# Turning the gated values of SwiGLU with DMA transposes of two 16-bit planes instead of TensorE transposes

## The chip, the core and the metric

The kernel runs on one core of one Trainium2 chip. The metric is device time in microseconds (us) of one execution, the median of several runs. A profiled execution of the same kernel gives a trace of every instruction on TensorE (PE, with its weight loads as PEld), VectorE (DVE), ScalarE (ACT), GpSimd (POOL), and of the DMA queue that SyncE (SP) issues into.

## What is computed

A two-layer encoder over 256 tokens of width 1024, in float32. Each layer adds half a SwiGLU block, a mixer (attention) and another half SwiGLU block to x:

```python
def swiglu(h, w_gate, w_up, w_down):
    return (jax.nn.silu(h @ w_gate) * (h @ w_up)) @ w_down

def reference(x, ...):
    for layer in range(DEPTH):                      # DEPTH = 2
        h = rms_norm(x, ffn1_norm[layer])
        x = x + 0.5 * swiglu(h, ffn1_w_gate[layer], ffn1_w_up[layer], ffn1_w_down[layer])
        h = rms_norm(x, mix_norm[layer])
        x = x + (even_mixer if layer % 2 == 0 else odd_mixer)(h, ...)
        h = rms_norm(x, ffn2_norm[layer])
        x = x + 0.5 * swiglu(h, ffn2_w_gate[layer], ffn2_w_up[layer], ffn2_w_down[layer])
    return rms_norm(x, final_norm)
```

The hidden width of SwiGLU is 2816. The gated values, `silu(h @ w_gate) * (h @ w_up)`, come out with tokens on the partitions, and the product with `w_down` needs the hidden index on the partitions: each 128x128 block of them has to be turned.

## The kernel before

**Tiles.** The 256 tokens are two row tiles of 128 (`tt` 0 and 1). A float32 product is made of three TensorE products: operands are split into a high part and a low part (`hi`, `lo` of the weights; `th`, `tl` of the normalised input; `g_h`, `g_l` of the gated values), and `mm` issues hi*hi, lo*hi and hi*lo at lines 460 to 462, each 128x512. One such triple is called a step below.

**Stages.** Stages 0, 2, 3 and 5 are the four SwiGLU blocks, 1 and 4 the mixers. A SwiGLU stage goes through five chunks of 512 hidden columns and a last one of 256 (`FF_MIXED`): gate products for both row tiles, up products for both, then `silu` on ACT (line 649) and `glu` on DVE (line 654). After all chunks come the products with `w_down`.

**Strassen chunks.** In each stage one or two chunks (`SEVEN`: chunk 2 in stages 0 and 5, chunks 1 and 3 in stages 2 and 3), and some pairs of the down products, are made with seven instead of eight products. They need sums of weights: DVE makes `two` and rewrites `raw` (line 389), ACT makes `shi` and DVE `slo` from them, beside the usual `hi` and `lo`. So DVE does more work there for fewer steps of TensorE. The parts of the finished chunk are put together and gated on DVE at lines 754 to 792 (`L773` is the gating).

**Weights.** SP issues loads of the weights into three buffers `raw` (`load`, line 373), ACT rounds them to `hi` (line 468), DVE subtracts to `lo` (line 471). At most seven pairs `wp` and three pairs `sum` are held, so ACT waits for TensorE's last use of a pair when it is far ahead.

**What sets the order.** Every engine takes its instructions in the order in which the program writes them. Work that is not a product is written as generators: `tick` is called once after every step and advances each generator whose count of ticks has run out (`yield n` waits n ticks), then makes the next weight part when the due rate says so. Loops that only wait for a generator call `tick(False)`, which advances generators without a step of TensorE between them.

**The place of the change.** `glu` writes the gated tile `m`, waits `GLU_WAIT` = 14 ticks, and `transposed` turns its four blocks on TensorE into a PSUM bank `tp` (`turned`, line 538). ACT then copies out `quarters` (blocks that a Strassen pair of the down product needs, lines 680 and 683) and `g_h` (line 468), and DVE makes `g_l` (line 471).

Of the kernel before, what the change touches and what calls it, by code (L numbers as in the profile page):

```python
# [9 lines left out]
F32 = mybir.dt.float32  # L10
F32R = mybir.dt.float32r
BF16 = mybir.dt.bfloat16
AF = mybir.ActivationFunctionType
# [4 lines left out]
P = 128  # L18
# [7 lines left out]
ROWS = T // GRID_W  # L26
# [16 lines left out]
RAWS = 3  # L43
# [10 lines left out]
GLU_WAIT = 14  # L54
# [8 lines left out]
ROWS, ROWS_WAIT = 4, 30  # L63
# [64 lines left out]
class Split:  # L128
# [3 lines left out]
    def __init__(self, raw, uses, first=False, narrow=False, kind="wp", then=None):  # L132
        self.raw, self.first, self.narrow, self.kind, self.then = raw, first, narrow, kind, then
# [67 lines left out]
class Trunk:  # L201
# [161 lines left out]
    def load(self):  # L363
# [12 lines left out]
        if kind == "strassen":  # L376
            self.coming(self.strassen(raw, halves))
        else:
            views = [halves(raw[:, k, :]) for k in range(nk)] if w == D else [raw[:, k : min(k + 2, nk), :] for k in range(0, nk, 2)]
            self.coming([Split(view, uses, n == 0, kind == "narrow") for n, view in enumerate(views)])  # L380
# [5 lines left out]
    def strassen(self, raw, halves):  # L386
# [7 lines left out]
        def all_sums():  # L394
# [7 lines left out]
            Split(second[:, 0:1, :], [1], True, then=all_sums),  # L402
            Split(first, [1]),
            Split(first, [1], kind="sum"),
            Split(second, [1], kind="sum"),
# [3 lines left out]
    def supply(self):  # L409
# [6 lines left out]
        if split.parts is None:  # L416
            if split.first:
                self.load()
# [116 lines left out]
    def turned(self, src, n=4):  # L535
# [3 lines left out]
        return tb  # L539

# [95 lines left out]
    def ffn(self):  # L636
# [14 lines left out]
        def glu(tt, f0, w, u, s):  # L651
# [83 lines left out]
        def seven_gates(f0, w, pairs7):  # L735
# [12 lines left out]
            def common():  # L748
# [4 lines left out]
                w = self.t([P, 512], "silu", 2)  # L753
# [8 lines left out]
            def first_gate():  # L762
# [3 lines left out]
                s = self.t([P, 512], "silu", 2)  # L766
# [5 lines left out]
            def up(tt, o, u, s):  # L772
                nc.vector.scalar_tensor_tensor(o, u, self.now.r[tt], s, op0=ALU.mult, op1=ALU.mult)  # L773
                yield GLU_WAIT
                yield from transposed(tt, f0, w, o)
# [59 lines left out]
        for ci, w in enumerate(FF_CHUNKS):  # L835
# [11 lines left out]
            for tt in range(NT):  # L847
                g = both[tt] if self.now.n + ci == 0 else self.project(self.ready(tt), G, tags[tt])
                S.append(self.t([P, 512], "silu", 2))
# [8 lines left out]
        for tt in range(NT):  # L858
            both = self.project(self.now.hT[tt], V, "s")
            s = self.t([P, 512], "silu", 2)  # L860
# [49 lines left out]
        def combine():  # L910
# [5 lines left out]
            c = self.t([P, 512], "silu", 2)  # L916
# [3 lines left out]
            v = self.t([P, 512], "silu", 2)  # L920
# [5 lines left out]
            y = self.t([P, 512], "silu", 2)  # L926
# [328 lines left out]
    def fetch_row(self, rel, n):  # L1255

        row = self.little([P, 2, ROW], "rows", ROWS)
# [200 lines left out]
    def run(self):  # L1458
# [50 lines left out]
        self.rows = []  # L1509
        self.start(self.first_rows(a["c_rel_bias"][0]))  # L1510
        self.phase(self.ffn)
        self.next_stage()
        self.phase(self.odd, a["c_rel_bias"][0])
        self.next_stage()
# [31 lines left out]
```

## Time and profile before

| what | value |
|---|---|
| median of 3 runs | 954.43 us (954.36 to 954.94) |
| profiled execution, its own time | 954.08 us |
| its span in the trace | 952.3 us |
| PE busy | 939.0 us (99%) |
| DVE busy | 790.9 us (83%) |
| ACT busy | 583.2 us (61%) |
| DMA share of 16 engines, queue of SP | 53.9% |
| TensorE transposes of `glu` | 176, in 40 groups of four and 8 of two |

"Busy" is the union of an engine's instructions. PE's matmuls overlap in the records: one of 128x512 is shown with 0.39 us, and the next one starts about 0.23 us after it. Times of rows are counted from the span's start. A row of the timeline reads: start, duration, engine, line, operation, out<-in, shapes, count, and in brackets the idle time of the engine before it and what ended it.

### The profile page before, as it was taken

How to read it: one execution, taken by the hardware profiler on the slowest of the kernel's cores; microseconds unless marked ns; L12 is line 12 of the kernel's file. 1: busy time of each engine (PE TensorE's matmuls, PEld its weight loads, DVE VectorE, ACT ScalarE, POOL GpSimd, SP SyncE). 2: the span in 40 equal slices, each digit the busy share in tenths (PEclk: the TensorE clock that was granted, in tenths of full speed). 3: DMA queues.
4: the chain of work that ended last, by engine and by line, in shares of the span. 5: the costliest groups of instructions: out<-in, count | busy, mean ns of one | idle time of the engine just before them, and what ended most of it. 6: DMA issues, size and time to landing. Idle time of an engine off the chain costs nothing.

```text
span 952.3 us, 12568 instructions
## 1 busy us (share of the span) xinstructions
PE 939.0 (99%) x4575; PEld 770.2 (81%) x4575; DVE 790.9 (83%) x1228; ACT 583.2 (61%) x995; POOL 94.4 (10%) x152
## 2 busy tenths in 40 slices
PE   9999999999999999999999999999999999999997
PEld 6888888877878888888888888888878888888786
DVE  6989778788869998787978888888878697896797
ACT  7555655477787565645646556557777585555453
POOL 1120000063410000000100000006130000000001
PEclk9999999999999999999999999999999999999999
DMA  8737555644425665556446575664634365466261
GB/s 300 265 128 239 204 191 173 210 136 102 118 89 177 220 209 190 207 191 225 153 153 213 159 245 174 226 214 161 185 97 159 101 219 179 151 229 238 88 243 45
DMA packets 82751, 171.63 MB, mean 180 GB/s; under 512 B 4096, under 2 KB 17152, under 8 KB 82688
## 3 DMA queue, kind: packets, MB, share of 16 engines
q1 hardware_dynamic: 82112, 170.04, 53.9%
q8 instruction: 36, 0.59, 0.3%
q10 hardware_dynamic: 576, 0.79, 0.2%
q14 instruction: 27, 0.22, 0.1%
HBM read 169.76 MB, written 1.05 MB: 179 GB/s over the span
## 4 chain that ended last, share of the span: by engine, by line
PE 89%; DVE 5%; ACT 3%; issue 1%; DMA 1%; POOL 0%; POOLq 0%; ACTq 0%; DVEq 0%
PE s L461 12%; PE s L462 12%; PE s L460 12%; PE pj L460 12%; PE pj L462 11%; PE pj L461 11%; PE tp L538 2%; PE o L460 2%; PE o L462 2%; PE o L461 2%; DVE lo L471 2%; PE o L1019 2%; PE tp L1098 1%; PE tp L460 1%; PE tp L462 1%
## 5 line engine op out<-in xcount | busy, mean ns | idle before, releaser
L471 DVE TENSOR_TENSOR lo<-raw,hi 128x1024 fp32r<-128x1024 f32 (+1 forms) x372 | 374.2, 1027 | 64.2 <-ACT hi L468 61.4
L468 ACT ACTIVATE hi<-raw 128x1024 fp32r<-128x1024 f32 (+1 forms) x372 | 317.9, 890 | 76.4 <-PE s L462 26.3
L460 PE MATMUL s<-hi,th 128*128 128x512 f32 x373 | 149.1, 400 | 0.4 <-ACT hi L468 0.4
L460 PE MATMUL pj<-hi,th 128*128 128x512 f32 x367 | 146.7, 400 | 0.0
L461 PE MATMUL s<-lo,th 128*128 128x512 f32 x373 | 145.8, 391 | 0.3 <-DVE lo L471 0.2
L462 PE MATMUL s<-hi,tl 128*128 128x512 f32 x373 | 145.9, 391 | 0.0
L461 PE MATMUL pj<-lo,th 128*128 128x512 f32 x367 | 143.2, 390 | 0.1
L462 PE MATMUL pj<-hi,tl 128*128 128x512 f32 x367 | 143.3, 390 | 0.0
L461 PEld LDWEIGHTS s<-lo,th 128*128 128x128 f32 x373 | 70.2, 188 | 15.0 <-DVE lo L471 1.5
L462 PEld LDWEIGHTS s<-hi,tl 128*128 128x128 f32 x373 | 70.0, 188 | 14.9
L460 PEld LDWEIGHTS s<-hi,th 128*128 128x128 f32 x373 | 70.1, 188 | 13.9 <-ACT hi L468 0.6
L462 PEld LDWEIGHTS pj<-hi,tl 128*128 128x128 f32 x367 | 68.9, 188 | 14.7
L460 PEld LDWEIGHTS pj<-hi,th 128*128 128x128 f32 x367 | 69.0, 188 | 13.9 <-issue 0.9
L461 PEld LDWEIGHTS pj<-lo,th 128*128 128x128 f32 x367 | 69.1, 188 | 13.4 <-DVE lo L471 0.5
L480 POOL TENSOR_TENSOR rstd<-var,mhalf 128x1 f32<-128x1 f32 (+2 forms) x16 | 17.1, 1069 | 590.5 <-ACT th L501 309.0
L468 ACT ACTIVATE shi<-two 128x1024 fp32r<-128x1024 f32 x30 | 31.8, 1059 | 39.4 <-DVE two L389 39.3
L460 PE MATMUL s<-hi,g_h 128*128 128x512 f32 (+1 forms) x131 | 52.1, 398 | 0.0
L471 DVE TENSOR_TENSOR slo<-raw,shi 128x1024 fp32r<-128x1024 f32 x30 | 36.7, 1223 | 18.3 <-ACT shi L468 18.3
L468 ACT ACTIVATE shi<-raw 128x1024 fp32r<-128x1024 f32 x30 | 31.7, 1057 | 32.5 <-PE s L462 22.0
L468 ACT ACTIVATE g_h<-tp 128x512 fp32r<-128x512 f32 (+2 forms) x48 | 25.7, 537 | 42.4 <-DVE quarters L686 28.1
L462 PE MATMUL s<-hi,g_l 128*128 128x512 f32 (+1 forms) x131 | 51.0, 389 | 0.0
L461 PE MATMUL s<-lo,g_h 128*128 128x512 f32 (+1 forms) x131 | 50.8, 388 | 0.0
(483 smaller groups left out, 1668.4 us busy)
## 6 DMA issues: line engine op xcount, KB each, us to landing
raw<-in_ffn_w_down SPq DMA_DIRECT2D x44, 1024.0 KB, 5.0
raw<-in_ffn_w_up SPq DMA_DIRECT2D x28, 1024.0 KB, 5.2
raw<-in_ffn_w_gate SPq DMA_DIRECT2D x26, 1024.0 KB, 5.1
raw<-in_ffn_w_gate SPq DMA_DIRECT2D x35, 512.0 KB, 4.1
raw<-in_ffn_w_up SPq DMA_DIRECT2D x32, 512.0 KB, 5.1
raw<-in_odd_w_qkv SPq DMA_DIRECT2D x12, 1024.0 KB, 5.3
raw<-in_even_w_in SPq DMA_DIRECT2D x4, 1024.0 KB, 5.2
raw<-in_even_w_out SPq DMA_DIRECT2D x8, 512.0 KB, 6.0
```

The costliest lines, as they stand in the source:

```text
L460: mm(ps, h, wh, start=first, stop=False)
L461: mm(ps, h, wl, start=False, stop=False)
L462: mm(ps, l, wh, start=False, stop=last)
L468: self.nc.scalar.activation(hi, src, AF.Copy)
L471: self.nc.vector.tensor_tensor(lo, src, hi.bitcast(F32), op=ALU.subtract)
L480: nc.gpsimd.tensor_tensor(r[:, :n], v[:, :n], self.mhalf[:, :n], op=ALU.pow)
L538: self.nc.tensor.transpose(tb[:, i * P : (i + 1) * P], src[:, i * P : (i + 1) * P], self.ident)
L1019: self.nc.tensor.matmul(O[64 * s : 64 * s + 64, i * P : i * P + P], v(b0 + i, s, kc), pT[s][:, i, kc, :], start=(kc == 0), stop=(kc == 1),)
L1098: nc.tensor.transpose(tb[:, o : o + P], p[:, i, kc * P : kc * P + P], self.ident)
```

## The change

`turned` on TensorE is replaced, for the gated values alone, by `turned_over`. ACT copies the float32 tile `m` as 16-bit numbers into a new tile of the `silu` pool, all lower halves first and all upper halves behind (two planes of 512 columns). SP issues one DMA transpose of those 128x1024 16-bit numbers back into `m`, in eight blocks of 128x128. ACT copies `m` back into the other tile with lower and upper halves side by side again. The turned tile is then in SBUF, not PSUM, and `quarters` and the split into `g_h` and `g_l` read it there. `transposed` now runs as a generator of its own, so that waiting for the gating tasks no longer waits for the turning. The waits change from 14 ticks to 1 tick ahead of the first copy, 1 ahead of the DMA and 8 ahead of the second copy.

Two more edits go with it. The load of the next weights is written when the last part of a `raw` buffer has been made, not when the first part of a later one begins, and the first two such loads are left out because five were issued at the start; a load so stands in SP's queue near the time its buffer comes free. And the rows of the relative bias get a pool of their own, since `silu` has three buffers instead of two.

```diff
-GLU_WAIT = 14
+GLU_WAIT = 1
+TURN_WAIT = [1, 8]
...
+        self.ahead = len(FIRST) - RAWS
...
         if split.parts is None:
-            if split.first:
-                self.load()
...
+        if split.last and sl.stop == split.raw.shape[1]:
+            if self.ahead:
+                self.ahead -= 1
+            else:
+                self.load()
...
+    def turned_over(self, m, w):
+
+        two = self.t([P, 512], "silu", 3)
+        planes, back = (t.bitcast(U16)[:, : 2 * w] for t in (two, m))
+        self.nc.scalar.copy(planes.rearrange("p (h c) -> p h c", h=2), back.rearrange("p (c h) -> p h c", h=2))
+        yield TURN_WAIT[0]
+        self.nc.sync.dma_start_transpose(back.rearrange("p (j t) -> p j t", t=P), planes)
+        yield TURN_WAIT[1]
+        self.nc.scalar.copy(planes.rearrange("p (c h) -> p h c", h=2), back.rearrange("p (h c) -> p h c", h=2))
+        yield 1
+        return two
...
             nc.vector.scalar_tensor_tensor(m[:, :w], u[:, :w], self.now.r[tt], s[:, :w], op0=ALU.mult, op1=ALU.mult)
-            yield GLU_WAIT
-            yield from transposed(tt, f0, w, m)
+            self.spawn(transposed(tt, f0, w, m), GLU_WAIT)
...
         def transposed(tt, f0, w, m):
             n = w // P
-            tb = self.turned(m, n)
-            yield 1
+            tb = yield from self.turned_over(m, w)
...
             def up(tt, o, u, s):
                 nc.vector.scalar_tensor_tensor(o, u, self.now.r[tt], s, op0=ALU.mult, op1=ALU.mult)
-                yield GLU_WAIT
-                yield from transposed(tt, f0, w, o)
+                self.spawn(transposed(tt, f0, w, o), GLU_WAIT)
+                yield 1
...
-        row = self.little([P, 2, ROW], "rows", ROWS)
+        row = self.row_pool.tile([P, 2, ROW], F32, tag="rows", name=self.name("rows"), bufs=ROWS)
```

Three places of the order matter for what follows. The first is ACT in stage 2, at the end of chunk 0 and the start of the Strassen chunk 1. In the rows, `hi` and `shi` are weight parts, `g_0_h` the high part of the turned values of chunk 0 (one row for each row tile), the other `g_` and `k` rows sums of the input for the Strassen chunk. Before:

```order
L468 ACTIVATE hi_3152<-raw_2877 128x512
L468 ACTIVATE hi_3173<-raw_2877 128x1024
L468 ACTIVATE g_12_h_3183<-shi_3024 128x384
L468 ACTIVATE shi_3189<-two_3160 128x1024
L468 ACTIVATE g_16_h_3200<-shi_3024 128x384
L468 ACTIVATE k16h_3206<-slo_3072 128x384
L468 ACTIVATE g_0_h_3214<-tp_3209 128x512
L468 ACTIVATE k14h_3218<-slo_3072 128x384
L468 ACTIVATE shi_3230<-raw_2877 128x1024
L468 ACTIVATE hi_3244<-raw_2977 128x512
L468 ACTIVATE g_0_h_3255<-tp_3237 128x512
```

The same stretch of ACT in the changed kernel; COPY at L551 takes the halves apart, COPY at L555 puts them together:

```order
L474 ACTIVATE hi_3138<-raw_3068 128x512
L551 COPY silu_3156<-glu_3151 128x1024
L474 ACTIVATE hi_3162<-raw_3068 128x1024
L474 ACTIVATE g_12_h_3172<-shi_3010 128x384
L474 ACTIVATE shi_3178<-two_3146 128x1024
L474 ACTIVATE g_16_h_3189<-shi_3010 128x384
L551 COPY silu_3194<-glu_3192 128x1024
L555 COPY silu_3156<-glu_3151 128x2x512
L474 ACTIVATE g_0_h_3198<-silu_3156 128x512
L474 ACTIVATE k16h_3202<-slo_3055 128x384
L474 ACTIVATE k14h_3207<-slo_3055 128x384
L555 COPY silu_3194<-glu_3192 128x2x512
```

Behind these rows follow `g_0_h_3211` and `shi_3223`. The first COPY stands ahead of the last `hi` of its buffer, and both second COPYs stand ahead of the `shi` that was ninth before; between the COPY that feeds the second DMA transpose and the COPY that needs its result stand four short instructions, because a loop there waits for sums and advances generators without steps of TensorE.

The second is DVE at the same place in the changed kernel, where `slo_3224` is made from the `shi` just named:

```order
L672 SCALAR_TENSOR_TENSOR glu_3192<-pj_3141,rstd_3030,silu_3094 128x512
L477 TENSOR_TENSOR g_16_l_3190<-shi_3010,g_16_h_3189 128x384
L477 TENSOR_TENSOR g_0_l_3199<-silu_3156,g_0_h_3198 128x512
L477 TENSOR_TENSOR k16l_3203<-slo_3055,k16h_3202 128x384
L477 TENSOR_TENSOR k14l_3208<-slo_3055,k14h_3207 128x384
L477 TENSOR_TENSOR g_0_l_3212<-silu_3194,g_0_h_3211 128x512
L477 TENSOR_TENSOR slo_3224<-raw_3068,shi_3223 128x1024
```

Before, the second `g_0_l` stood five rows behind that `slo`; now both `g_0_l` stand ahead of it.

The third is ACT behind the Strassen chunk of stage 2, where `glu_3400` and `glu_3356` are its gated tiles, in the changed kernel:

```order
L551 COPY silu_3422<-glu_3400 128x1024
L474 ACTIVATE hi_3424<-raw_3354 128x1024
L804 ACTIVATE glu_3356<-glu_3356,rstd_3030 128x512
L551 COPY silu_3447<-glu_3356 128x1024
L667 ACTIVATE silu_3442<-pj_3391,rstd_2940 128x512
L474 ACTIVATE hi_3454<-raw_3354 128x1024
L474 ACTIVATE hi_3467<-raw_3378 128x1024
L555 COPY silu_3422<-glu_3400 128x2x512
```

Before, ACT went from the activation (`L788` there) straight to `silu` and three `hi`; now a COPY that needs the second gated tile stands between.

More of the change, by code (lines that the diff above doesn't have):

```diff
@@ L128, with __init__ @@
 class Split:
-    def __init__(self, raw, uses, first=False, narrow=False, kind="wp", then=None):
-        self.raw, self.first, self.narrow, self.kind, self.then = raw, first, narrow, kind, then
+    def __init__(self, raw, uses, last=False, narrow=False, kind="wp", then=None):
+        self.raw, self.last, self.narrow, self.kind, self.then = raw, last, narrow, kind, then
         n = raw.shape[1]
@@ L401, in strassen @@
         splits = [
[L402 removed]
+            Split(second[:, 0:1, :], [1], then=all_sums),
             Split(first, [1]),
             Split(first, [1], kind="sum"),
[L405 removed]
+            Split(second, [1], True, kind="sum"),
         ]
@@ L1508, in run @@
         self.next_stage()
[L1509 to L1514, printed above, removed]
+        with self.tc.tile_pool(name="rows", bufs=1, reuse_waits="tile") as self.row_pool:
+            self.rows = []
+            self.start(self.first_rows(a["c_rel_bias"][0]))
+            self.phase(self.ffn)
+            self.next_stage()
+            self.phase(self.odd, a["c_rel_bias"][0])
+            self.next_stage()
         self.phase(self.ffn)
```

17 lines of the change are left out of this document (9 added, 8 removed).

## The prediction

> **What bounds the kernel now.** I read the page's engine table and the shares of the chain that ended last first, then the timeline around a group of transposes, then the stretches in which DVE is fullest.
>
> ```profile
> span 952.3 us, 12568 instructions
> PE 939.0 (99%) x4575; PEld 770.2 (81%) x4575; DVE 790.9 (83%) x1228; ACT 583.2 (61%) x995; POOL 94.4 (10%) x152
> PE 89%; DVE 5%; ACT 3%; issue 1%; DMA 1%; POOL 0%; POOLq 0%; ACTq 0%; DVEq 0%
> ```
>
> PE is busy nearly without a gap and carries the chain, so time taken from PE is time taken from the end, as long as nothing else comes last. DVE has 17% left on the average, but not everywhere (stage 2, first 54 us; columns PE, PEld, DVE, ACT, POOL):
>
> ```profile
> 291.00:345.00 54.00, 53.67 (x244) 44.03 (x243) 52.39 (x63) 33.72 (x43) 0.00 (x0) 1.00 0.60 201
> ```
>
> Here DVE is busy 52.4 of 54 us: PE and DVE end together, and whatever makes DVE wait is a delay.
>
> **What is removed.** One group of four transposes in the stream of PE, and all of them in the tile's view:
>
> ```profile
> 35.00 0.39 PE L462 MATMUL s<-hi,tl 128*128 128x512 f32 x1
> 35.23 0.60 PE L538 MATMUL tp<-mats,glu 128*128 128x128 f32 x4
> 35.59 0.48 PE L460 MATMUL s<-hi,th 128*128 128x512 f32 x1
> 35.90 0.39 PE L461 MATMUL s<-lo,th 128*128 128x512 f32 x1
> L538 PE MATMUL tp<-mats,glu x176: 270/271/328, 35.2 to 897.4; 128*128 128x128 f32 x176
> ```
>
> A matmul follows the one ahead after 0.23 us (35.00 to 35.23). From 35.00 to 35.90 there are three such steps less one, 0.45 us, without the group; 0.90 are seen, so four transposes cost 0.45 us, 0.112 each (the 271 ns of the last row is a record that overlaps its neighbours). 176 x 0.112 = **19.7 us** come off PE. [...]
>
> **What is added on ACT.** Per tile of 512 columns two copies of 128x1024 16-bit numbers, for the tiles of 256 columns two of 128x512. Nearest rows:
>
> ```profile
> L468 ACT ACTIVATE hi<-raw 128x1024 fp32r<-128x1024 f32 x230 | 234.9, 1052 | 59.4 <-PE s L462 20.4 <-PE pj L462 17.8 <-DMA raw<-in_ffn_w_up 12.2
> L468 ACT ACTIVATE hi<-raw 128x512 fp32r<-128x512 f32 x142 | 85.1, 626 | 17.0 <-PE s L462 6.0 <-DMA raw<-in_ffn_w_down 4.1 <-DMA raw<-in_odd_w_qkv 3.8
> L468 ACT ACTIVATE g_h<-tp 128x512 fp32r<-128x512 f32 x30 | 17.8, 596 | 19.3 <-DVE quarters L686 10.7 <-PE tp L538 8.6
> ```
>
> No row has 16-bit operands on ACT. Same element count: 1.05 us; if two 16-bit numbers went as one, 0.63. I take 1.05, the row with the same number of elements. 80 x 1.05 + 16 x 0.63 = 94 us more on ACT, 677 in all, some 70%: as a sum it hides. `g_h` now reads SBUF, 626 for 596 ns, 48 times: 1.4 us, hidden too.
>
> **What is added on the queue of SP.** 48 DMA transposes, 11 MB to the 170 there. Nearest rows for one of 256 KB from issue to landing:
>
> ```profile
> out<-shi SPq DMA_DIRECT2D x2, 256.0 KB, 2.7
> rows<-in_c_rel_bias SPq DMA_DIRECT2D x16, 109.5 KB, 5.5
> last_gain<-in_final_norm SPq DMA_DIRECT2D x1, 512.0 KB, 7.2
> ```
>
> 2.7 is a plain transfer out of SBUF into an empty queue, 7.2 the longest of these. I take 6, near `rows`, which also goes in small pieces beside the weight loads. [...]
>
> The loads are written later, at the end of a buffer's use. I cost this at nothing: SP already stands waiting for exactly that event,
>
> ```profile
> SPq L373 <- DVE lo L471: 435.5, 106, 14.0
> ```
>
> so a load leaves when DVE frees its buffer, before and after. A DMA transpose ahead of it in the queue holds it until ACT's copy is done; the other two buffers cover that, and without them ACT's next `hi` would wait. The pool for the bias rows moves no work of the SwiGLU stages: nothing.
>
> **What is moved: where ACT now waits.** Before, ACT had `hi` and `shi` ready ahead of DVE, and `g_h` waited for PE only 14 ticks on. Now each first COPY waits on ACT for DVE's `glu`, with the `hi` and `shi` of the next weights queued behind it, on which DVE waits; each second COPY waits for a DMA. Stage 2, chunk 0, where the order was shown:
>
> ```profile
> 299.39 1.06 ACT L468 ACTIVATE hi<-raw 128x1024 fp32r<-128x1024 f32 x1 [3.12 <-PE pj L462]
> 301.40 0.74 DVE L654 SCALAR_TENSOR_TENSOR glu<-pj,rstd,silu 128x512 f32<-128x512 f32 x1
> 301.52 0.53 ACT L468 ACTIVATE g_h<-shi 128x384 fp32r<-128x384 f32 x1 [1.06 <-DVE shi L723]
> 301.95 1.05 ACT L468 ACTIVATE shi<-two 128x1024 fp32r<-128x1024 f32 x1
> 303.19 1.22 DVE L471 TENSOR_TENSOR slo<-two,shi 128x1024 fp32r<-128x1024 f32 x1
> 304.33 0.55 DVE L471 TENSOR_TENSOR g_l<-shi,g_h 128x384 fp32r<-128x384 f32 x1
> 304.80 0.75 DVE L654 SCALAR_TENSOR_TENSOR glu<-pj,rstd,silu 128x512 f32<-128x512 f32 x1
> 304.82 1.05 ACT L468 ACTIVATE shi<-raw 128x1024 fp32r<-128x1024 f32 x1
> 307.46 1.22 DVE L471 TENSOR_TENSOR slo<-raw,shi 128x1024 fp32r<-128x1024 f32 x1
> 319.25 1.22 DVE L471 TENSOR_TENSOR lo<-raw,hi 128x1024 fp32r<-128x1024 f32 x1
> 320.65 0.40 PE L461 MATMUL s<-lo,th 128*128 128x512 f32 x1
> ```
>
> Before, the last `lo` here ends at 320.47 and PE reads it at 320.65: 0.2 us to spare, and DVE runs from 307.46 to there with 0.2 us idle. Now, in the new order: `glu` ends 302.14, COPY 303.19, `hi` 304.24, `g_12_h` (0.53) and `shi` 305.8, `slo` 305.8 to 307.0, `g_12_l` (0.55) and `glu` end 308.3 (305.55 before). The second COPY of planes ends 309.4, the first COPY back 310.4, `g_0_h` (0.60) and two `k` rows (as `g_12_h`) 312.1. The second DMA transpose, issued at 309.4, lands at 315.4; COPY back 316.4, `g_0_h` 317.0, `shi` 318.1. So `slo` starts at 318.1 instead of 307.46, 10.6 late; less the two spare 0.2 us and the 0.6 us of `g_0_l`, which moved ahead of it, PE waits **9.6 us**. With 2.7 us for the DMA and 0.63 for a COPY the same walk gives 5.1.
>
> Stage 5, chunk 1, before its Strassen chunk:
>
> ```profile
> 805.11 0.74 DVE L654 SCALAR_TENSOR_TENSOR glu<-pj,rstd,silu 128x512 f32<-128x512 f32 x1
> 812.36 0.74 DVE L654 SCALAR_TENSOR_TENSOR glu<-pj,rstd,silu 128x512 f32<-128x512 f32 x1
> 815.89 0.41 DVE L686 TENSOR_TENSOR quarters<-tp,quarters 128x256 f32<-128x256 f32 x1
> 816.98 0.69 DVE L471 TENSOR_TENSOR g_l<-tp,g_h 128x512 fp32r<-128x512 f32 x1 [0.67 <-ACT g_h L468]
> 818.95 0.69 DVE L471 TENSOR_TENSOR k4l<-quarters,k4h 128x512 fp32r<-128x512 f32 x1 [0.76 <-ACT k4h L468]
> 825.08 0.39 PE L460 MATMUL s<-hi,th 128*128 128x512 f32 x1
> 825.51 0.50 PE L461 MATMUL s<-lo,th 128*128 128x512 f32 x1
> ```
>
> COPY and `hi` behind the first `glu` (805.85) end at 807.95, which puts DVE 2.2 behind; the second `glu` ends 815.3, its COPY 816.35, the DMA lands 822.35, COPY back and `quarters` 823.7, and L686 starts 7.8 late. The 1.4 us that DVE idles in the next rows take some of it, and I round down: **6 us** (low end, worked as above, 2.4). PE has nothing to spare here: the last matmul starts 0.43 after the one ahead, not 0.23.
>
> Six Strassen chunks, six such stretches. Stage 0 I take as the mean of the two, 8. The first of stage 3 has room,
>
> ```profile
> 500.71 1.06 ACT L468 ACTIVATE shi<-raw 128x1024 fp32r<-128x1024 f32 x1 [3.57 <-PE pj L462]
> ```
>
> ACT waits for PE 3.6 us just where the delay would arrive: 0. The second ones of stages 2 and 3 were not walked; 4 each, halfway between none and 8. Sum **31.6**.
>
> Behind a Strassen chunk (stage 2):
>
> ```profile
> 335.92 0.67 ACT L649 ACTIVATE silu<-pj,rstd 128x512 f32<-128x512 f32 x1
> 336.49 2.94 ACT L468 ACTIVATE hi<-raw 128x1024 fp32r<-128x1024 f32 x3
> 337.82 0.75 DVE L773 SCALAR_TENSOR_TENSOR glu<-silu,rstd,glu 128x512 f32<-128x512 f32 x1
> 338.49 4.63 DVE L471 TENSOR_TENSOR lo<-raw,hi 128x1024 fp32r<-128x1024 f32 x4
> 340.68 0.39 PE L461 MATMUL s<-lo,th 128*128 128x512 f32 x1
> ```
>
> The `hi` that ran at 336.49 now stands behind the COPY that needs the `glu` of 337.82: COPY ends 339.6, `silu` (0.67) 340.3, `hi` 341.3, `lo` 342.6 instead of 339.7. PE read it at 340.68: 1.9 late, and 3.4 if the first COPY ahead adds its own 1.5. I take 2.5 for each of six, **15 us**. Everywhere else I cost the COPYs at nothing: `lo` is ready some us ahead there, and where that lead is under 2 us the same price would come again.
>
> **The sum**, on the profiled execution's own 954.08 (0.4 under the median of 954.43, so the same): 954.08 - 19.7 + 31.6 + 15 = **981**. With the low ends (5.1, 2.4, 4, 1, 1, and 1.5 behind each of six) 957; with 7.2 us for the DMA, 8 in both unwalked places and 3.4 behind each chunk 998.
>
> **Rivals.** *The lead holds* (other side): ACT's 39% idle and the weights held ahead swallow the waits, and PE only loses its transposes: 934. For it speaks stage 3's 3.6 us above; against it the 52.4 of 54 us. It decides once the stalls of all stretches stay under 19.7, 3.3 for each Strassen chunk, against the 7.8 that I work out. *The stalls just eat the gain*: 952 to 957. *The DMA transpose is slow*: beyond 6 us each more microsecond falls on the five stretches; 12 us give 981 + 30 = 1011. [...] *Loads come late* behind the DMA transposes: ACT already waits 12.2 us for `w_up` (row above), 11 us more would make 992, inside the range.
>
> **How the numbers follow.** 981 and its range 957 to 998, with late loads, 0.64; lead holds, 0.16; eaten, 0.05; slow DMA 0.15. A change under 0.2%, 952.5 to 956.3, cannot be told from none. Faster 0.17, same 0.04, slower 0.79. The range for 8 in 10 cuts the ends of both far cases: 945 to 1012.
>
> **What would show it.** Right: no `tp<-mats,glu`, PE busy lower by about 18 us while its idle time grows by tens, in front of `lo` and `slo` rows of the Strassen chunks; 96 COPYs near 1.05 us; ACT waiting for the DMA at the second COPY; DVE waiting longer for `hi` and `shi`. Wrong: PE without gaps there, which means that the DMA lands within some 3 us and that the COPYs are short; or landings over 10 us, which makes it worse.

## The result, and the profile after

The changed kernel takes 1038.81 us in the median of 4 runs (1036.33 to 1041.97), the kernel before 954.68 beside it (954.36 to 955.08): ratio 1.0883, 95% interval 1.0852 to 1.0913, 84 us slower. The direction was forecast, the size was not: 27 us were expected, and the time lies outside the range of 945 to 1012. The profiled execution took 1039.17 us, with a span of 1037.4.

The page of the changed kernel: the span, busy times, the granted clock in 40 slices, and the shares of the chain that ended last.

```profile
span 1037.4 us, 12414 instructions
PE 957.1 (92%) x4399; PEld 764.5 (74%) x4399; DVE 792.6 (76%) x1228; ACT 681.5 (66%) x1091; POOL 92.6 (9%) x152
PEclk9998999999999989999999998999999999999999
DVE 31%; PE 28%; ACT 18%; DMA 12%; issue 9%; SPq 0%; POOL 0%; ACTq 0%; POOLq 0%; DVEq 0%
```

PE carried 89% of the chain and now carries 28%. DVE, ACT and the DMA hand the end from one to the other, and no engine is full: PE 92%, DVE 76%, ACT 66%. That fits engines that wait for each other in turn; the experiments below test it.

Groups by line and shape on ACT (count, then busy time, mean of one, and after the second bar the idle time ahead of them with what ended it):

```profile
L474 ACT ACTIVATE hi<-raw 128x1024 fp32r<-128x1024 f32 x230 | 234.2, 1049 | 24.0 <-PE s L468 8.6 <-DMA raw<-in_ffn_w_gate 6.3 <-DMA raw<-in_ffn_w_up 4.3
L555 ACT COPY silu<-glu 128x1024 uint16<-128x1024 uint16 x40 | 53.8, 1345 | 15.8 <-DMA glu<-silu 15.6
L551 ACT COPY silu<-glu 128x1024 uint16<-128x1024 uint16 x40 | 41.9, 1046 | 102.5 <-DVE glu L672 69.6 <-DVE glu L789 32.9
```

The first COPY costs 1.05 us as assumed; the second, which writes every other 16-bit number, 1.35. ACT stands 102.5 us ahead of the first COPYs, waiting for DVE's gating. And `hi` now waits 8.6 us for PE where the same row before had 20.4 and 17.8: ACT is seldom ahead of PE any more.

The DMA transposes, in the view of issues (count, median us from issue to landing) and in that of the tile (ns of SP's own issue, minimum, median, maximum):

```profile
glu<-silu SPq DMA_TRANSPOSE x48, 3.2
```
```profile
L553 SPq DMA_TRANSPOSE glu<-silu x48: 1188/1232/2886, 27.1 to 981.3; - x48
```

They land after 3.2 us in the median (2.4 to 6.7 by the same view), not 6. They go in small pieces as assumed: the page counts 50688 DMA packets under 512 B, that of the kernel before 4096.

**Where the 84 us lie.** I took every product that both kernels issue (1238 steps; the first matmul of each), and subtracted its start before from its start after. This lateness grows as follows. The places are those of the prediction; their borders, in us of the kernel before, stand in the first column. Each figure is the growth over the place, gains of removed transposes included. Another choice of borders moves a few us between the rows of a column, not its sum. The last three columns are kernels of the experiments below, with the same borders.

| place | forecast | changed kernel | waits, no copying (`short`) | copying, no waits (`work`) | DMA alone (`onlydma`) |
|---|---|---|---|---|---|
| ahead of the six Strassen chunks and in them (60 to 79, 292 to 330, 359 to 374, 487 to 512, 541 to 556, 809 to 835) | 31.6 | 36.7 | 16.2 | 9.5 | 6.6 |
| behind them (from each end above to 137, 359, 409, 541, 591, 893) | 15 | 32.0 | 0.5 | -5.5 | -13.4 |
| ends of the four stages (137 to 191, 409 to 462, 591 to 644, from 893) | 0 | 16.1 | 2.0 | 3.5 | -1.2 |
| all the rest | -19.7 | -0.5 | -1.9 | -2.0 | -1.7 |
| sum | 27 | 84.3 | 16.8 | 5.5 | -9.7 |

The six stretches ahead are, in order of time, 8.7, 6.8, 6.7, -1.0, 6.2 and 9.3 us late (forecast 8, 9.6, 4, 0, 4, 6). So 57 us are missing from the forecast: 5.1 in the six stretches ahead, 17.0 behind the chunks, 16.1 at the ends, and 19.2 of a gain that does not show in the rest. Many of the removed transposes stand inside the first three places, so part of that gain did arrive there, and the stalls are larger by as much than the figures of these places.

The walked place, stage 2 ahead of chunk 1, in the timeline of the changed kernel (start, duration, instruction, idle time ahead and what ended it):

```profile
319.20 0.74 DVE L672 SCALAR_TENSOR_TENSOR glu<-pj,rstd,silu 128x512 f32<-128x512 f32 x1
319.97 1.05 ACT L551 COPY silu<-glu 128x1024 uint16<-128x1024 uint16 x1 [5.81 <-DVE glu L672]
320.93 1.05 ACT L474 ACTIVATE hi<-raw 128x1024 fp32r<-128x1024 f32 x1
322.01 1.23 DVE L477 TENSOR_TENSOR lo<-raw,hi 128x1024 fp32r<-128x1024 f32 x1 [2.07 <-ACT hi L474]
325.82 1.05 ACT L551 COPY silu<-glu 128x1024 uint16<-128x1024 uint16 x1 [2.07 <-DVE glu L672]
326.77 1.34 ACT L555 COPY silu<-glu 128x1024 uint16<-128x1024 uint16 x1
329.96 1.35 ACT L555 COPY silu<-glu 128x1024 uint16<-128x1024 uint16 x1 [0.35 <-DMA glu<-silu]
331.87 1.04 ACT L474 ACTIVATE shi<-raw 128x1024 fp32r<-128x1024 f32 x1
332.94 1.23 DVE L477 TENSOR_TENSOR slo<-raw,shi 128x1024 fp32r<-128x1024 f32 x1 [0.25 <-ACT shi L474]
332.96 0.50 PE L466 MATMUL s<-shi,th 128*128 128x512 f32 x1 [1.27 <-ACT shi L474]
```

The order does what the walk said. ACT is idle for 5.8 us with a `hi` behind the COPY, and DVE, which makes the `glu` that ACT waits for, is then idle 2.1 us for that `hi`. The last `slo` starts at 332.94 against 307.46 before, 25.5 later. Of that, 17.8 was there at the first `glu` of the place (319.20 against 301.40 before), so 7.7 arose here, forecast 10.6. It arose by other waits than the walk had: there ACT stood 3.3 us for the DMA (312.1 to 315.4), here 0.35, and more ahead of the first COPYs.

Behind a Strassen chunk, where 2.5 us had been allowed, the timeline of the changed kernel:

```profile
359.35 1.05 ACT L551 COPY silu<-glu 128x1024 uint16<-128x1024 uint16 x1 [4.79 <-DVE glu L789]
360.31 1.05 ACT L474 ACTIVATE hi<-raw 128x1024 fp32r<-128x1024 f32 x1
361.39 1.23 DVE L477 TENSOR_TENSOR lo<-raw,hi 128x1024 fp32r<-128x1024 f32 x1 [1.47 <-ACT hi L474]
364.84 1.04 ACT L551 COPY silu<-glu 128x1024 uint16<-128x1024 uint16 x1 [2.86 <-DVE glu L789]
365.79 0.68 ACT L667 ACTIVATE silu<-pj,rstd 128x512 f32<-128x512 f32 x1
366.37 1.99 ACT L474 ACTIVATE hi<-raw 128x1024 fp32r<-128x1024 f32 x2
367.45 2.36 DVE L477 TENSOR_TENSOR lo<-raw,hi 128x1024 fp32r<-128x1024 f32 x2 [2.64 <-ACT hi L474]
367.47 0.80 PE L466 MATMUL s<-hi,th 128*128 128x512 f32 x1 [3.19 <-ACT hi L474]
```

The `glu` of each row tile stands on DVE behind the operations that put the Strassen chunk together, so ACT stands twice, 4.8 and 2.9 us. In the second stand two weight parts and a `silu` queue up, and PE waits 3.2 us. The forecast had followed one `hi` at this place, not two stands on ACT in a row.

At the ends of stages 3 and 5 PE waits for `lo` (2.0 and 2.3 us at most), at those of stages 0 and 2 for `x`, to which DVE adds the products (3.5 and 2.7). Stage 0, in the timeline of the changed kernel:

```profile
188.77 2.01 ACT L474 ACTIVATE hi<-raw 128x1024 fp32r<-128x1024 f32 x2 [4.97 <-PE s L468]
201.71 0.66 PE L522 MATMUL tp<-mats,x 128*128 128x128 f32 x4 [3.49 <-DVE x L609]
```

ACT waits 5.0 us for PE here, so it is ahead, and it is DVE that comes late; a stretch of 3.41 us at half the clock follows (202.75 to 206.16).

### The profile page after: what moved, and what is told of

It reads as the page before. It is cut to its first block, busy times and chain, and to the rows that moved or that the text cites. A ratio compares the mean times of both kernels' runs of the same rounds, so it can differ in the third digit from the quotient of the medians.

```text
span 1037.4 us, 12414 instructions
## 1 busy us (share of the span) xinstructions
PE 957.1 (92%) x4399; PEld 764.5 (74%) x4399; DVE 792.6 (76%) x1228; ACT 681.5 (66%) x1091; POOL 92.6 (9%) x152
## 2 busy tenths in 40 slices
DMA packets 129343, 183.16 MB, mean 177 GB/s; under 512 B 50688, under 2 KB 63744, under 8 KB 129280
## 3 DMA queue, kind: packets, MB, share of 16 engines
HBM read 169.76 MB, written 1.05 MB: 165 GB/s over the span
## 4 chain that ended last, share of the span: by engine, by line
DVE 31%; PE 28%; ACT 18%; DMA 12%; issue 9%; SPq 0%; POOL 0%; ACTq 0%; POOLq 0%; DVEq 0%
DVE lo L477 12%; ACT hi L474 7%; DMA glu<-silu 7%; PE pj L466 5%; PE pj L468 4%; ACT silu L555 4%; PE pj L467 4%; DVE raw L392 3%; DVE two L392 2%; DVE slo L477 2%; PE s L467 2%; PE s L468 2%; PE s L466 2%; DMA raw<-in_ffn_w_up 2%; DVE g_l L477 2%
## 5 line engine op out<-in xcount | busy, mean ns | idle before, releaser
L467 PE MATMUL s<-lo,th 128*128 128x512 f32 x373 | 151.4, 406 | 18.8 <-DVE lo L477 18.8
L466 PE MATMUL s<-hi,th 128*128 128x512 f32 x373 | 150.3, 403 | 17.9 <-ACT hi L474 14.7
L468 PE MATMUL s<-hi,tl 128*128 128x512 f32 x373 | 149.0, 399 | 0.0
L467 PE MATMUL pj<-lo,th 128*128 128x512 f32 x367 | 145.3, 396 | 2.1 <-DVE lo L477 1.9
L551 ACT COPY silu<-glu 128x1024 uint16<-128x1024 uint16 (+1 forms) x48 | 46.8, 975 | 112.9 <-DVE glu L672 79.9
L466 PEld LDWEIGHTS s<-hi,th 128*128 128x128 f32 x373 | 71.6, 192 | 37.7 <-ACT hi L474 19.7
L468 PEld LDWEIGHTS s<-hi,tl 128*128 128x128 f32 x373 | 72.2, 193 | 14.5
L555 ACT COPY silu<-glu 128x1024 uint16<-128x1024 uint16 (+1 forms) x48 | 59.9, 1248 | 15.9 <-DMA glu<-silu 15.6
L477 DVE TENSOR_TENSOR g_l<-silu,g_h 128x512 fp32r<-128x512 f32 (+2 forms) x48 | 29.6, 618 | 29.9 <-ACT g_h L474 29.9
```

The source lines that it names most:

```text
L466: mm(ps, h, wh, start=first, stop=False)
L467: mm(ps, h, wl, start=False, stop=False)
L468: mm(ps, l, wh, start=False, stop=last)
L477: self.nc.vector.tensor_tensor(lo, src, hi.bitcast(F32), op=ALU.subtract)
L551: self.nc.scalar.copy(planes.rearrange("p (h c) -> p h c", h=2), back.rearrange("p (c h) -> p h c", h=2))
L555: self.nc.scalar.copy(planes.rearrange("p (c h) -> p h c", h=2), back.rearrange("p (h c) -> p h c", h=2))
```

## The experiments

The theories: *ACT and DVE wait for each other* (the first COPY waits for DVE's `glu`, with weight parts for DVE behind it); *ACT has too much work* (some 100 us of copying, wherever it stands); *the DMA is late*; *the moved loads cost*. Where one run is named there is no interval. The changed kernel is the one that each diff starts from. The diffs leave one edit out: only the kernels of *the first COPY without its wait*, of *both COPYs, no DMA* and of *PE kept from standing still* keep the changed kernel's pool, in which the COPYs' tile takes a buffer of `silu`; in the others `silu` has two buffers again, and the COPYs' tile, where there is one, a pool of its own. The five kernels that copy or turn something other than the gated values, or leave the turning out, do not compute the reference: they measure time alone.

**The moved loads alone.** The turning stays on TensorE, 14 ticks behind `glu`; the loads and the pool for the bias rows are as changed.

```diff
-            self.spawn(transposed(tt, f0, w, m), GLU_WAIT)      # GLU_WAIT = 1
+            yield GLU_WAIT                                      # GLU_WAIT = 14
+            yield from transposed(tt, f0, w, m)
...
-            tb = yield from self.turned_over(m, w)
+            tb = self.turned(m, n)
+            yield 1
```

> The later loads and the pool for the bias rows, with the turning left on TensorE as before (14 ticks). Theory 'ACT and DVE wait for each other' (ACT's first COPY waits for glu, the weight parts behind it are late, DVE waits for them), theory 'ACT has too much work' and theory 'the DMA is late' all expect no change, 953 to 956 us. If the moved loads cost part of the 84 us: above 960.

Measured 954.95 us against 954.67, ratio 1.0008 (0.9998 to 1.0018). The loads cost nothing, as forecast.

**The first COPY without its wait.** It copies a part of x that has long been ready; the DMA, which writes the gated tile, then waits for `glu` on SP.

```diff
-        self.nc.scalar.copy(planes.rearrange("p (h c) -> p h c", h=2), back.rearrange("p (c h) -> p h c", h=2))
+        ready = self.x[0].bitcast(U16)[:, : 2 * w]
+        self.nc.scalar.copy(planes.rearrange("p (h c) -> p h c", h=2), ready.rearrange("p (c h) -> p h c", h=2))
```

> The changed kernel, but the first COPY reads the input x instead of the gated tile, so that ACT does the same work and never waits for DVE at that place; SP's queue waits for glu instead (what is turned is then not the gated values). 'ACT and DVE wait for each other': the 113 us that ACT waits there go, and 40 to 60 us of the time come back, 980 to 1000. 'ACT has too much work': still above 1025. 'The DMA is late': still above 1025.

Measured 999.21 us (one run). The same work on ACT without the wait for `glu` gives 40 of the 84 us back. But 45 remain, so that wait is not the whole cause.

**Both COPYs, no DMA.** The second COPY reads the gated tile unturned.

```diff
-        self.nc.sync.dma_start_transpose(back.rearrange("p (j t) -> p j t", t=P), planes)
...
-        self.nc.scalar.copy(planes.rearrange("p (c h) -> p h c", h=2), back.rearrange("p (h c) -> p h c", h=2))
+        self.nc.scalar.copy(planes.rearrange("p (c h) -> p h c", h=2), back.rearrange("p (c h) -> p h c", h=2))
```

> The changed kernel without the DMA transposes: both COPYs stay, the second copies the gated tile unturned with the same strided output. 'ACT and DVE wait for each other' and 'too much work': 1020 to 1038, since ACT waited only 16 us for DMAs. 'The DMA is late': below 1000.

Measured 1021.21 us (one run): beside the COPYs the DMA's share is 18 us.

**The DMA, no COPYs.** SP transposes a constant tile into the gated tile behind `glu`, and the split reads the result.

```diff
-        self.nc.scalar.copy(planes.rearrange("p (h c) -> p h c", h=2), back.rearrange("p (c h) -> p h c", h=2))
-        self.nc.sync.dma_start_transpose(back.rearrange("p (j t) -> p j t", t=P), planes)
+        self.nc.sync.dma_start_transpose(back.rearrange("p (j t) -> p j t", t=P), self.minus.bitcast(U16)[:, : 2 * w])
...
-        self.nc.scalar.copy(planes.rearrange("p (c h) -> p h c", h=2), back.rearrange("p (h c) -> p h c", h=2))
...
-        return two
+        return m
```

> The DMA transposes without the COPYs: SP turns a constant tile into the gated tile once glu is written, and the split reads that (the values are not the gated ones). 'ACT and DVE wait for each other' and 'too much work': 936 to 955, since ACT's queue is as before. 'The DMA is late': above 980.

Measured 945.32 us (one run), 9 us faster than before. So a kernel can hide the DMA, issue and landing included, although ACT waits 76 us for it at the split (`quarters` and `g_h`, three rows of the waits view), and what is lost on the whole is lost only where the COPYs are there too. Even here the six stretches ahead lose 6.6 us, and 9 us, not 19.7, are left of the removed transposes.

**The waits without the copying.** Both COPYs keep their places and waits, but move 16 columns.

```diff
-        self.nc.scalar.copy(planes.rearrange("p (h c) -> p h c", h=2), back.rearrange("p (c h) -> p h c", h=2))
-        self.nc.sync.dma_start_transpose(back.rearrange("p (j t) -> p j t", t=P), planes)
+        self.nc.scalar.copy(two[:, :16], m[:, :16])
+        self.nc.sync.dma_start_transpose(back.rearrange("p (j t) -> p j t", t=P), self.minus.bitcast(U16)[:, : 2 * w])
...
-        self.nc.scalar.copy(planes.rearrange("p (c h) -> p h c", h=2), back.rearrange("p (h c) -> p h c", h=2))
+        self.nc.scalar.copy(two[:, 16:32], m[:, :16])
```

> Both waits of ACT stay (the first COPY waits for DVE's glu, the second for the DMA), but each COPY moves 16 columns of float32, not the whole tile, and the DMA turns a constant tile; the split reads the DMA's result directly. So ACT has the waits of the changed kernel without the 94 us of copying. If ACT and DVE waiting for each other is the cause by itself: the 40 us that came back when only that wait was taken away stay lost here, 945 + 40 = 985 us, between 975 and 995, and the idle time of lo in front of ACT's hi stays near 110 us. If it is the work on ACT that makes the waits cost anything: 945 to 955 us, as with the DMA alone.

Measured 973.00 us, ratio 1.0201 (1.0183 to 1.0220): both numbers missed. The waits by themselves cost 28 us above the DMA alone, and not 40; they also do not vanish.

**The copying without the waits.** Both COPYs at full size in their places, from a part of x that is ready.

```diff
-        self.nc.scalar.copy(planes.rearrange("p (h c) -> p h c", h=2), back.rearrange("p (c h) -> p h c", h=2))
-        self.nc.sync.dma_start_transpose(back.rearrange("p (j t) -> p j t", t=P), planes)
+        self.nc.scalar.copy(planes.rearrange("p (h c) -> p h c", h=2), ready.rearrange("p (c h) -> p h c", h=2))
+        self.nc.sync.dma_start_transpose(back.rearrange("p (j t) -> p j t", t=P), self.minus.bitcast(U16)[:, : 2 * w])
...
-        self.nc.scalar.copy(planes.rearrange("p (c h) -> p h c", h=2), back.rearrange("p (h c) -> p h c", h=2))
+        self.nc.scalar.copy(planes.rearrange("p (c h) -> p h c", h=2), ready.rearrange("p (h c) -> p h c", h=2))
```

> Both COPYs stay on ACT at their full size and in their places, but each copies a part of x that has long been ready, and the DMA turns a constant tile into the gated tile, which the split reads. So ACT does the copying (some 115 us) and its COPYs wait for neither glu nor the DMA. If the copying by itself delays the weight parts: most of the 54 us between the DMA alone (945) and the kernel whose first COPY does not wait (999) stays, 975 to 1000 us. If only waits cost: 945 to 957 us.

Measured 961.39 us, ratio 1.0075 (1.0061 to 1.0089), again between the two forecasts: 16 us above the DMA alone. So, above the DMA alone, waits cost 28, copying 16, and both together 94 (945.3 to 1038.8). Neither theory alone holds, and the sum of the two does not reach half. "Without the waits" holds for the COPYs: at the split ACT still waits 29 us for the DMA. What may join the two is seen in ACT's own time in one piece of the program, the 86 steps of stage 2 that begin at 291.03 us before. The windows view of the same products in four kernels (length, then busy time of PE, PEld, DVE, ACT, POOL), and ACT's waits in each window. Before:

```profile
291.03:352.39 61.36, 61.03 (x279) 50.15 (x278) 59.69 (x71) 38.78 (x48) 0.00 (x0) 1.00 0.61 206
```
```profile
ACT hi L468 <- PE pj L462: 5.7, 4, 3.1
ACT shi L468 <- PE pj L462: 2.2, 1, 2.2
```

The kernel with the copying alone:

```profile
290.53:353.16 62.63, 59.43 (x259) 48.19 (x258) 56.56 (x67) 45.56 (x55) 0.00 (x0) 1.00 0.67 207
```
```profile
ACT hi L474 <- PE pj L468: 2.1, 1, 2.1
```

The kernel with the waits alone:

```profile
292.78:361.17 68.39, 63.27 (x259) 50.38 (x258) 59.32 (x70) 37.28 (x55) 0.00 (x0) 0.95 0.65 202
```
```profile
ACT turn L551 <- DVE glu L672: 12.3, 4, 6.0
ACT turn L551 <- DVE glu L789: 7.6, 2, 4.8
```

The changed kernel, with DVE's waits as well:

```profile
308.82:382.38 73.56, 64.84 (x260) 50.80 (x258) 55.49 (x65) 45.01 (x53) 0.00 (x0) 0.93 0.55 172
```
```profile
ACT silu L551 <- DVE glu L672: 10.0, 3, 5.8
ACT silu L551 <- DVE glu L789: 7.7, 2, 4.8
```
```profile
DVE lo L477 <- ACT hi L474: 13.4, 9, 3.0
DVE g_l L477 <- ACT g_h L474: 4.2, 2, 2.6
```

Before, ACT waited 7.9 us for PE: it was ahead by so much. Its other waits (10.0 for DVE, 2.8 for loads, by the same view) come to 9 to 14 us in each kernel. With the copying alone ACT is busy 6.8 us longer (45.56 less 38.78), its waits for PE fall by 5.8, and the piece grows by 1.3. With the waits alone ACT stands 19.9 us for `glu`, its waits for PE are gone, and the piece grows by 7.0. With both, 6.2 of work and 17.7 of waits come in, the 7.9 can be spent only once, and the piece grows by 12.2.

Busy time and idle time fill a piece on any engine, so such sums show where the time went and not yet why. What speaks for ACT's lead over PE is that it goes first, and not only here: over the whole kernel `hi` and `shi` wait 73 us for PE before, 21 with the copying alone, 9 with the waits alone and 12 in the changed kernel. ACT works in order, so its work and its waits add up; in the changed kernel it is busy or waiting for DVE for some 71 of the 73.6 us, at 61% busy. DVE reads the same way, busy 55.5 us and waiting 17.9 for ACT (1.5 before): each stands for the other, and ACT not for PE.

So the runs show that the COPYs on ACT cost the time, by their waits and by their work; that the two cost more together because they draw on one lead is argued from these rows. In the piece the excess is 3.9 us (12.2 against 1.3 and 7.0). One more thing sets the changed kernel apart from the two halves, the pool that its COPYs share with `silu`: ACT waits 5.7 us in all for a buffer there (`silu` L667 for `g_l`), 1.4 of them in this piece, and in the halves not at all. The changed kernel with a pool of its own for the COPYs was not run.

**The COPYs on GpSimd.** Nothing of ACT's stands behind the COPYs on their own engine; the split, which stays on ACT, follows 6 ticks after the second.

```diff
-        self.nc.scalar.copy(planes.rearrange("p (h c) -> p h c", h=2), back.rearrange("p (c h) -> p h c", h=2))
+        self.nc.gpsimd.tensor_copy(planes.rearrange("p (h c) -> p h c", h=2), back.rearrange("p (c h) -> p h c", h=2))
...
-        self.nc.scalar.copy(planes.rearrange("p (c h) -> p h c", h=2), back.rearrange("p (h c) -> p h c", h=2))
+        self.nc.gpsimd.tensor_copy(planes.rearrange("p (c h) -> p h c", h=2), back.rearrange("p (h c) -> p h c", h=2))
```

> The full change, with both COPYs on GpSimd instead of ACT, and the split 6 ticks after the second COPY; what is computed is the same as before. GpSimd waits for glu and for the DMA, and no weight part stands behind it. If ACT's waits and its copying are the cause: 945 us of the DMA alone plus what the longer way from glu to g_h costs, 945 to 965 us. If the DMA or the longer way is what counts, g_h waits for GpSimd with hi and shi behind it and the time stays above 985 us. A copy of 128x1024 16-bit numbers on GpSimd is taken as 2 to 3 us, from its row of 1.1 us for 128x384.

Measured 992.92 us, ratio 1.0408 (1.0382 to 1.0434): 46 us better than on ACT, but inside the second forecast, above 985, by which `g_h` waits for GpSimd with weight parts behind it. That it does:

```profile
ACT quarters L697 <- POOL turn L556: 54.2, 13, 6.8
ACT g_h L475 <- POOL turn L556: 33.4, 8, 8.7
```

With a third row of 15.7 ACT stands 103 us for the second COPY. DVE pays too, as its group of the largest `lo` and its timeline beside a COPY show:

```profile
L478 DVE TENSOR_TENSOR lo<-raw,hi 128x1024 fp32r<-128x1024 f32 x230 | 297.5, 1323 | 24.2 <-ACT hi L475 24.1
```
```profile
902.16 1.34 POOL L556 COPY turn<-glu 128x1024 uint16<-128x1024 uint16 x1 [2.51 <-DMA glu<-turn]
902.17 4.62 DVE L478 TENSOR_TENSOR lo<-raw,hi 128x1024 fp32r<-128x1024 f32 x3 [0.76 <-ACT hi L475]
```

A `lo` takes 1.32 us in the mean, where the kernel before has 1.22 (275.7 us for 230), and three of them beside a COPY 4.62 us, where 1.1 from start to start (four take 4.63 us in the kernel before, at 338.49) would give 3.4 to 3.5. DVE's busy time rises from 790.9 to 846.0 us. Why a `lo` is slower there, no run here shows. How the 48 us above the DMA alone divide between ACT's waits and the slower DVE, no run here tells.

**The COPYs on ACT, but later.** The first one 10 ticks behind `glu`, and the turning awaited as before the change (the same edit stands in `up` of the Strassen chunks).

```diff
-GLU_WAIT = 1
+GLU_WAIT = 10
...
-            self.spawn(transposed(tt, f0, w, m), GLU_WAIT)
+            yield GLU_WAIT
+            yield from transposed(tt, f0, w, m)
```

> The full change with the COPYs on ACT, but the first COPY is written 10 ticks after glu instead of 1, and the turning is waited for at the end of a stage's gating tasks, as before the change. By the theory that ACT waits for glu with weight parts behind it, most waits for glu go (114 us of ACT idle time ahead of the first COPY in the changed kernel, under 50 here) and the time comes near the 999 us of the kernel whose COPY does not wait, 995 to 1015 us. If the copying on ACT is what counts, wherever it stands: 1025 to 1045 us.

Measured 1029.78 us, ratio 1.0791 (1.0774 to 1.0808). ACT's idle time ahead of the first COPY went as forecast (4.7 us instead of 112.8), and the time hardly moved: it lies in the second forecast, and the first theory does not give it. ACT's longest wait, and one of PE's, in this kernel:

```profile
ACT turn L555 <- DMA glu<-turn: 86.1, 28, 6.8
```
```profile
PE s L466 <- DVE glu L672: 23.9, 6, 6.0
```

The later COPY moved the wait to the second COPY, where ACT now stands 86 us for the DMA, and since the turning is awaited, loops without products advance it with nothing on PE. So one wait was traded for others. Since this kernel changes two things at once, it does not tell the copying from the awaited turning.

**PE kept from standing still.** The granted clock falls to a half in 12 places of the changed kernel. Here 214 matmuls of zeros fill 85% of each of PE's waits of 0.7 us and more.

```diff
+        for n in range(FILL_HI.get(at, 0)):
+            mm(ps, self.zero16[:, :P], idle, start=first and n == 0, stop=False)
-        mm(ps, h, wh, start=first, stop=False)
+        mm(ps, h, wh, start=first and at not in FILL_HI, stop=False)
+        for n in range(FILL_LO.get(at, 0)):
+            mm(ps, self.zero16[:, :P], idle, start=False, stop=False)
```

> The changed kernel, with 214 matmuls of zeros on PE put into the places where it waited 0.7 us and more, by some 85% of each wait, added to the sum that is open there, so that TensorE does not stand still. If the half-clock stretches that follow PE's waits (12 places, 14 of 3.41 us) cost what PE does less in them, some 23 us in all: they go, and the time falls to 1014 to 1029 us. If ACT and DVE come last in those stretches anyway: the granted clock rises from 0.974 to 0.99 or more, and the time stays at 1034 to 1043 us.

Measured 1033.85 us, ratio 1.0830 (1.0815 to 1.0845), with the granted clock up from 0.974 to 0.995. Of some 23 us of lost clock 5 come back, as the second forecast has it: the slower PE is mostly hidden behind ACT and DVE. What the zeros themselves cost PE is in this figure too.

**Only where it does no harm.** Two kernels turn by DMA in 9 chunks of plain products only, 18 of 48 tiles, with the COPYs on GpSimd or on ACT (there 4 ticks behind `glu`). Five of the nine do border on a Strassen chunk, other than the first expectation says. Of the chunks of 512 columns the ones left out are the Strassen chunks and the chunk right ahead of each; only the one ahead of stage 3's first is in.

```diff
+OVER = {0: (0, 3, 4), 2: (4,), 3: (0, 4), 5: (0, 3, 4)}     # stage: chunks
...
+            if over:
+                self.spawn(transposed(tt, f0, w, m, True), GLU_WAIT)
+                return
+            yield TENSOR_WAIT                                   # 14
+            yield from transposed(tt, f0, w, m, False)
```

> The DMA transposes only in the chunks of plain products that do not stand next to a Strassen chunk (chunks 0, 3 and 4 of stages 0 and 5, 4 of stage 2, 0 and 4 of stage 3: 18 of 48 tiles), with the COPYs on GpSimd; the other tiles are turned on TensorE as before. If all losses lie next to the Strassen chunks: 18 tiles by four transposes by 0.112 us are 8 us of PE time that come back, 946 to 950 us. If chunk 0 of stage 0 loses 6 us, as it did with all COPYs on GpSimd, 950 to 956. If plain chunks lose elsewhere too: 956 to 965.

> The same 18 tiles by DMA, with the COPYs on ACT and the first one 4 ticks behind glu, so that ACT seldom waits for it. If ACT's lead over PE in plain chunks covers two COPYs and a DMA for each tile: 946 to 950 us. If it doesn't, each of 9 chunks loses 1 to 3 us, against 0.9 gained: 955 to 970 us.

Measured 965.24 us on GpSimd, ratio 1.0117 (1.0103 to 1.0131), and 958.79 on ACT, 1.0037 (1.0024 to 1.0051). The first lies just above the last of its forecasts, the second in the second forecast. By the lateness of the same products the one on ACT loses 6 to 7 us around chunk 0 of stage 0 and 4.5 behind chunk 4 of stage 3, and gains 1 to 2 in most others. So a last kernel leaves out these two and chunk 0 of stage 5:

```diff
-OVER = {0: (0, 3, 4), 2: (4,), 3: (0, 4), 5: (0, 3, 4)}
+OVER = {0: (3, 4), 2: (4,), 3: (0,), 5: (3, 4)}
```

> As the kernel with 18 tiles turned by DMA and the COPYs on ACT, but without the chunks that lost time there by the start of the same products in the two traces: chunk 0 of stage 0 (6 us), chunk 4 of stage 3 (4 us) and chunk 0 of stage 5 (0.3 us). Left are chunks 3 and 4 of stages 0 and 5, 4 of stage 2 and 0 of stage 3, 12 tiles of 48. If each stretch keeps what it showed (2 us, 1, 1 and 2.3 gained, 1 lost elsewhere): 948 to 951 us, faster than before. If the gain in one place is eaten by a wait that only moved: 953 to 957 us.

Measured 951.15 us against 954.52, ratio 0.9962 (0.9949 to 0.9976): 3.4 us or 0.4% faster than the kernel before, just above the forecast of 948 to 951. Its busy times:

```profile
PE 935.0 (98%) x4527; PEld 766.5 (81%) x4527; DVE 792.6 (83%) x1228; ACT 606.9 (64%) x1019; POOL 91.4 (10%) x152
```

12 tiles by four transposes by 0.112 us are 5.4 us of PE time. In the profiled execution 4.1 had arrived by the end of stage 3, 2.0 were lost again in stage 4, 1.9 gained in stage 5 and 2.3 lost at the start of its down products; why, I did not follow further. Of the kernels that compute the gated values this is the only one that beats both.

## Why the prediction was wrong, point by point

- **Direction right, mechanism in part.** DVE waits for `hi`, 138 us instead of 61 by the waits view; ACT waits at both COPYs; and PE waits in front of weight parts next to the Strassen chunks. But the walk made the wait for the DMA the long one, and ACT waits 15.6 us for DMAs in the whole kernel against 112.8 for `glu`.
- **The six stretches ahead: right in the sum, 36.7 for 31.6, and partly by luck.** The two walked places came out at 6.8 for 9.6 and 9.3 for 6, the two set at 4 without a walk at 6.7 and 6.2. The two errors in the prices (DMA 3.2 for 6 us, second COPY 1.35 for 1.05) have opposite signs. The slow DMA of the rivals did not happen, nor did loads come late: `hi` waits 4.3 us for `w_up`, before 12.2.
- **"I take 2.5 for each of six, 15 us": mis-sized, 32.0.** One `hi` was followed behind one COPY. There are two stands of ACT, one for each row tile.
- **"Everywhere else I cost the COPYs at nothing": the step that failed in kind, 16.1 at the ends of the stages alone.** The reason given was that `lo` is ready some us ahead there. The prediction walked each place against the times of before, as if that lead were whole at each. In the piece above ACT's lead over PE is one store for the whole stretch: the copying alone uses 5.8 of 7.9 us, and the waits alone all of it. At the ends themselves this is not shown, and at that of stage 0 it is not so: ACT is ahead there, and PE waits for `x` behind a late DVE. Why that place loses 5.3 us in the changed kernel and 3.9 with the zeros on PE, but 0 to 1.3 in the seven others with DMA or COPYs in every chunk, I did not settle.
- **"176 x 0.112 = 19.7 us come off PE": nearly right for PE, wrong for the end.** With the DMA alone PE is busy 922.9 us, 16.1 less, and the time falls by 9. In the changed kernel only 0.5 us of gain are left in the stretches where nothing else was charged. The likely reason is that a shorter PE gains nothing where PE waits for DVE and ACT; the prediction set the whole gain against the stalls as if they lay in different places.
- **PE's busy time was to fall by 18 us and rose by 18.** Half-clock stretches make its records longer (a matmul of 128x512 is shown with 0.63 us from 339.38 on, at 0.50, and with 0.39 at 342.76, at full clock); the clock was not in the forecast at all. Filling PE's waits brought 5 us.
- **The rival that the lead holds** put the point of decision at 3.3 us for each Strassen chunk; ahead and behind together it was passed at all six, least at the first of stage 3 (3.6).

## What to carry to other kernels

Moving work from a full engine to one that is 61% busy was not free here (84 us longer), where that engine works in order and feeds the others: add up its busy time and its waits over a stretch, and compare what you add with the time in which it waits for the bottleneck, for that is its lead, and in the piece above it could be spent only once. A wait and work that cost little by themselves can cost twice their sum when they come together (here 94 us against 28 and 16). Where a change loses on the whole, the lateness of the same products in two traces shows the places where it gains, and keeping it there alone can turn the sign.

## What was not expected of the hardware

The clock. After stretches in which PE had waited much, the windows view of the changed kernel shows whole stretches of 3.41 us at half the clock (PEclk is the seventh figure, after the five engines' busy times):

```profile
332.46:335.88 3.42, 2.16 (x8) 1.58 (x9) 3.17 (x4) 1.92 (x3) 0.00 (x0) 1.00 0.11 13
335.88:339.29 3.41, 1.44 (x7) 0.88 (x6) 3.34 (x5) 2.89 (x4) 0.00 (x0) 1.00 0.79 294
339.29:342.70 3.41, 3.41 (x9) 2.65 (x9) 3.38 (x5) 0.77 (x2) 0.00 (x0) 0.50 0.24 26
342.70:346.11 3.41, 3.41 (x15) 2.53 (x14) 3.38 (x4) 3.02 (x4) 0.00 (x0) 1.00 0.75 282
```

Behind 3.41 us with PE busy 1.44 the next 3.41 us run at 0.50 (9 matmuls against 15 in the one after it), and behind 3.42 us with PE busy 2.16 the clock stays full. On the same grid of 3.41 us the stretches of this kernel right ahead of a drop have PE busy for 0.4 to 1.65 us; the least busy one that no drop follows has 1.73:

```profile
598.70:602.12 3.42, 1.65 (x6) 1.08 (x7) 3.12 (x4) 3.42 (x6) 0.00 (x0) 1.00 0.07 7
602.12:605.53 3.41, 3.41 (x10) 2.76 (x9) 3.41 (x4) 2.38 (x3) 0.00 (x0) 0.50 0.97 332
496.31:499.72 3.41, 1.73 (x8) 1.11 (x6) 3.34 (x6) 0.00 (x0) 0.00 (x0) 1.00 0.72 268
499.72:503.13 3.41, 2.42 (x13) 2.08 (x14) 3.41 (x7) 1.73 (x6) 0.00 (x0) 1.00 0.05 13
```

In this trace the border so lies between 1.65 and 1.73 us of PE's busy time, near half of a stretch. No wait as long as a stretch was needed: PE's longest single wait in the one from 335.88 was 2.0 us (up to 338.55), and the clock fell in the next. The changed kernel has 14 stretches at half the clock outside its end, the kernel before none.

A DMA transpose in SBUF (256 KB in 40 of the 48) lands in 3.2 us and takes SP 1.23 us to issue, both in the median, where a weight load takes 0.4 to 0.5 (0.37 to 0.47 in SP's rows from 20 to 60 us). And ACT needs 1.35 us to write 1024 16-bit numbers at a stride of two, 1.05 us to read them so.
